# Compressed probabilities as one 128-partition tile, gate rows padded to 128 partitions, and the mLSTM's diagonal mask added by VectorE, in a hybrid mLSTM and sparse-attention block

## The chip, the core and the metric

The kernel runs on one core of a Trainium2 chip. Its metric is the device time of one execution, in microseconds (us). Before the change it is 655.17 us, the median of three runs (654.78 to 655.3).

A core has several engines that work side by side, each with its own queue: TensorE (PE in the profile) multiplies matrices and writes to PSUM; PEld is the loading of its stationary operand, which overlaps with the matmuls; VectorE (DVE), ScalarE (ACT) and GpSimd (POOL) do elementwise work; SyncE (SP) issues the DMAs. An engine works through its own instructions in the order in which they stand, and waits on semaphores for those of others.

## What is computed

One decoder layer on 512 tokens of width 1024, in float32: RMSNorm, one wide input projection, two branches, gated merge, output projection, residual, RMSNorm. Cut to what the change touches:

```python
# NSA branch, per query block: attention on 31 compressed blocks, gated with g[..., 0]
s_c = einsum('bghqd,bgnd->bghqn', qr, kc) * scale
p_c = softmax(where(m_c, s_c, NEG)) * m_c
o_c = einsum('bghqn,bgnd->bghqd', p_c, vc)
return g[..., 0:1] * o_c + g[..., 1:2] * o_s + g[..., 2:3] * o_w

# mLSTM branch, per chunk: weights of the past by gates, causal inside a chunk
logD = a[..., :, None] - a[..., None, :] + li[..., None, :]
logD = where(causal, logD, -inf)
s = einsum('bhld,bhsd->bhls', qc, kc) * exp(logD - m_t[..., None])
```

## The kernel before, in words

Nearly all products are done to float32 accuracy by splitting an operand x into a high part `h` (x rounded to float32r) and a low part `l` = x - h. `split` makes both: ScalarE copies to `h`, VectorE subtracts. A product is then three matmuls: high x high, low x high, high x low (lines 156 to 158 in `mm3`, 198, 200 and 202 in `passes`). Weights arrive by DMA in a raw tile `wr` (three buffers) and are split to `wh` and `wl` (three buffers each).

The input projection's columns run as a stream of jobs: `Stream.step(n)` gives out the next n matmuls of the current projection job, and the code calls it between the pieces of the other work, so TensorE fills with projections what would be waiting. `tick` calls it in the attention. Behind the normalisation the instructions of each engine are placed by a scheduler, by what is ready when and which buffer comes free, so that an edit can move other instructions too.

The attention runs over 4 pairs of heads, c, in two halves hh, and over two branches b (selected and window). `compressed(c)` makes the compressed scores of a head pair in `psc`, a softmax `sc` in several VectorE steps, transposes `sc` by TensorE (L735) to 64 rows (2 heads x 32 blocks) and splits the result to `pch` and `pcl`, 64 partitions each. For each of the 8 pairs (c, hh) `first` opens the output bank `po` (one buffer) with two matmuls, the compressed values `VC` (64 rows: 2 x 32; columns: high and low) against `pch` (L849) and against `pcl` (L850). Then the selected and window products come on top (L792, L793), and `collect` reads `po` with ScalarE and VectorE (`oc`).

The mLSTM runs over 4 heads. Its gates' running values lie as rows in `ghl`: rows 0 to 3 the high parts, rows 32 to 35 the low ones, of 36 partitions. A matmul with the selector `sel` of a head broadcasts a row to all 128 partitions (L946 to `pgb`). A second one (L948 to `pgm`) is followed by one (L949) that adds, with an identity `idr`, the mask `dmr` of a 128x128 diagonal block to every block. Both lie in banks of the score pool `ps`, which has two. Then seven exponentials write `Dm`: the four diagonal blocks from `pgm`, the parts behind from `pgb`. For each of four key blocks the scores are made in a bank of `ps` (L156 to L158; 512, 384, 256 and 128 columns), multiplied into `Dm` by VectorE, split to `Sh` and `Sl`, and later multiplied with the values (L979 to L981).

Of the kernel before, what the change touches and what calls it, by code (L numbers as in the profile page):

```python
# [11 lines left out]
F32 = mybir.dt.float32  # L12
F32R = mybir.dt.float32r
I32 = mybir.dt.int32
AF = mybir.ActivationFunctionType
OP = mybir.AluOpType
AX = mybir.AxisListType.X

T = 512
D = 1024  # L20
NT = T // 128
# [15 lines left out]
CI, CTRI, CROT, CCAUS, CDM, CCM, CC01, CINV, CEND = np.cumsum(  # L37
    [0, 128, 128, 128, 512, 128, 128, 128, 8]
).tolist()
# [24 lines left out]
def build(  # L64
# [22 lines left out]
    pe, pool = nc.tensor, nc.gpsimd  # L87
    act, dve = Engine(nc.scalar, "act"), Engine(nc.vector, "dve")
    A = act.activation

    pers = ctx.enter_context(tc.tile_pool(name="pers", bufs=1))
# [3 lines left out]
    def bank(tag, bufs):  # L95
        return psum.tile([128, 512], F32, name=tag, tag=tag, bufs=bufs)

    PP = lambda: bank("pp", 3)
    PS = lambda: bank("ps", 2)
# [3 lines left out]
    def f(ap):  # L103
        return ap.bitcast(F32)

    cst = pers.tile([128, CEND], F32, name="cst")
    ident = cst[:, CI : CI + 128]
# [17 lines left out]
    def split(src, hi, lo, eng="a"):  # L125
        if eng == "a":
            A(hi, src, AF.Copy)
        elif eng == "p":
            pool.tensor_scalar(hi, src, 1.0, 1.0, OP.mult, OP.mult)
        else:  # L130
            dve.tensor_copy(hi, src)
        dve.tensor_tensor(lo, src, f(hi), OP.subtract)
# [94 lines left out]
    gates = pers.tile([128, NT, 24], F32, name="gates")  # L227
    li = pers.tile([128, NT, 4], F32, name="li")
    lf = pers.tile([128, NT, 4], F32, name="lf")
    ghl = pers.tile([36, T], F32R, name="ghl")  # L230
    sel = pers.tile([36, 4], F32R, name="sel")
    Fc = pers.tile([128, NT, 4], F32, name="Fc")
    cs = pers.tile([128, NT, 4], F32, name="cs")
    em = pers.tile([128, NT, 4], F32, name="em")
# [2 lines left out]
    np_ = nsa.__enter__()  # L237
# [4 lines left out]
    rp = tc.tile_pool(name="rope", bufs=2)  # L242
    rpp = rp.__enter__()
    KC = [np_.tile([128, 2, 2, 32], F32R, name=f"KC{g}") for g in range(2)]
    VC = [np_.tile([64, 2, 2, 64], F32R, name=f"VC{g}") for g in range(2)]

    with tc.tile_pool(name="ph0", bufs=2, side="right") as p0, tc.tile_pool(
        name="small", bufs=1, side="right"
# [210 lines left out]

    for t in KC + VC:  # L460
        pool.memset(f(t), 0.0)
# [95 lines left out]
    def compress_v(hd):  # L557
        pk = PS()
        pe.matmul(pk[:64, 0:64], hd, W2[1][:, 0, :], start=True, stop=True)
        for g in range(2):  # L560
            for hh in range(2):
                s = slice(hh * 32, hh * 32 + 32)
                split(pk[g * 32 : g * 32 + 32, 0:64], VC[g][s, hh, 0, :], VC[g][s, hh, 1, :])

    KK = [[np_.tile([128, 2, T], F32R, name=f"k{g}{i}") for i in range(2)] for g in range(2)]

# [18 lines left out]
    def query_heads(c):  # L585
        H, L, a = roped.pop(("q", c))
        q = rope_b(H, L, a)
        Th = []
        for hh in range(2):
            s = slice(hh * 64, hh * 64 + 64)  # L590
            o = slice((1 - hh) * 64, (1 - hh) * 64 + 64)
            t = rpp.tile([128, T], F32R, name="Th", tag=f"Th{hh}")
            A(t[s, :], q[s, :], AF.Copy)
            dve.tensor_tensor(t[o, :], q[s, :], f(t[s, :]), OP.subtract)
            Th.append(t)
        heads[c] = H, L, Th
# [91 lines left out]
    query_heads(0)  # L688
    stream.step(8)
    compress_v(u1)  # L690
    cmp_pool.__exit__(None, None, None)

    ap_ = tc.tile_pool(name="att", bufs=2)
    at = ap_.__enter__()
# [7 lines left out]
    comp = {}  # L702

    def compressed(c):
        g = c // 2
        H, L, _ = heads[c]
        psc = PP()
        kcv = KC[g].rearrange("p i g n -> p (i g n)")
        for qb in range(NT):
            qs, o = slice(qb * 128, qb * 128 + 128), qb * 128  # L710
            pe.matmul(psc[:, o : o + 128], H[:, qs], kcv, start=True, stop=False)
            pe.matmul(psc[:, o : o + 64], L[:, qs], kcv[:, 0:64], start=False, stop=True)
        sc = at.tile([128, NT, 2, 32], F32, name="sc", tag="sc", bufs=1)
        mx = at.tile([128, NT, 2], F32, name="mx", tag="mx")
        pscv = psc.rearrange("p (b i g n) -> p b i g n", b=NT, i=2, g=2)
        dve.tensor_tensor(
            sc, pscv[:, :, 0], cm.unsqueeze(2).broadcast_to([128, NT, 2, 32]), OP.add
        )
        dve.tensor_tensor(sc, sc, pscv[:, :, 1], OP.add)
        scf = sc.rearrange("p b g n -> p (b g) n")  # L720
        mxf = mx.rearrange("p b g -> p (b g)")
        dve.tensor_reduce(mxf, scf, AX, OP.max)
        dve.tensor_tensor(scf, scf, mxf.unsqueeze(2).broadcast_to([128, 8, 32]), OP.subtract)
        A(sc, sc, AF.Exp, scale=0.125)
        dve.tensor_reduce(mxf, scf, AX, OP.add)
        dve.reciprocal(mxf, mxf)
        dve.tensor_tensor(mx, mx, gv[:, :, 2 * c : 2 * c + 2, 0], OP.mult)
        dve.tensor_tensor(scf, scf, mxf.unsqueeze(2).broadcast_to([128, 8, 32]), OP.mult)
        dve.tensor_tensor(sc, sc, c01.unsqueeze(2).broadcast_to([128, NT, 2, 32]), OP.mult)
        yield  # L730
        yield
        yield
        ptc = PP()
        for qb in range(NT):
            pe.transpose(  # L735
                ptc[:64, qb * 128 : qb * 128 + 128], sc[:, qb].rearrange("p g n -> p (g n)"), ident
            )
        pch = at.tile([64, T], F32R, name="pch", tag="pch", bufs=1)
        pcl = at.tile([64, T], F32R, name="pcl", tag="pcl", bufs=1)
        split(ptc[:64, :], pch, pcl)  # L740
        comp[c] = pch, pcl

    def softmax_block(c, hh, b, qb, pss, P, st):
        n = (qb + 1) * 128
# [64 lines left out]
    def tick(n=FILL):  # L809
        stream.step(n)  # L810
        for gen in list(side):
            if next(gen, side) is side:
                side.remove(gen)

    def new_p():
        return (
            at.tile([128, 1280], F32, name="P", tag="P", bufs=3),
            at.tile([128, 3, NT], F32, name="st", tag="st", bufs=4),
        )

    side.append(compressed(0))
    pair = new_p(), new_p()
    for qb in range(NT):
# [3 lines left out]
    po = None  # L827
    for i, (c, hh, b) in enumerate(units):
        cur = pair[b]
        if b and i + 1 < 16:  # L830
            pair = new_p(), new_p()
        if i % 4 == 2 and c < 3:
            while ("q", c + 1) not in roped:
                stream.step(1)
            query_heads(c + 1)
            side.append(compressed(c + 1))
        if i == 1:
            side.append(mgate())
        for qb in range(NT):
            if i + 1 < 16:  # L840
                score(*units[i + 1], qb, pair)
            tick()
            if late:
                late.popleft()()
        if b == 0:

            def first(c=c, hh=hh):
                vc = VC[c // 2][:, hh].rearrange("p i d -> p (i d)")
                pe.matmul(po, vc, comp[c][0], start=True, stop=False)  # L849
                pe.matmul(po, vc, comp[c][1], start=False, stop=False)  # L850

            while late:
                late.popleft()()
            po = PO()
            first()
        for kb in range(NT):
            tt = ptrans(cur[0], kb)
            tick()

            def apply(c=c, hh=hh, b=b, kb=kb, po=po, tt=tt):  # L860
                pvmul(c, b, kb, po, *tt)
                if b == 1 and kb == 3:
                    collect(c, hh, po)

            late.append(apply)
            if len(late) > LAG:
                late.popleft()()
# [14 lines left out]
    sgp = ctx.enter_context(tc.tile_pool(name="sgp", bufs=4))  # L882
    mlp = tc.tile_pool(name="ml", bufs=1)
    mp = mlp.__enter__()
    idr = mp.tile([128, 128], F32R, name="idr")
    dmr = mp.tile([128, 128], F32R, name="dmr")
    dve.tensor_copy(idr, ident)
    dve.tensor_copy(dmr, cst[:, CDM : CDM + 128])
    qk, vv = {}, {}

    def conv(i, h, e):
# [49 lines left out]
    for h in range(4):  # L941
        (qh, ql), (kh, kl) = qk[0, h], qk[1, h]
        vh, vl = vv[h]
        pgb = PS()
        sl = sel[:, h : h + 1].broadcast_to([36, 128])
        pe.matmul(pgb, sl, ghl, start=True, stop=True)  # L946
        pgm = PS()
        pe.matmul(pgm, sl, ghl, start=True, stop=False)  # L948
        pe.matmul(pgm, idr, dmr.unsqueeze(1).broadcast_to([128, 4, 128]), start=False, stop=True)  # L949
        Dm = mp.tile([128, 1280], F32, name="Dm", tag="Dm")  # L950
        for sb in range(NT):
            o, n = KOFF[sb], 512 - sb * 128
            bias = cs[:, sb, h : h + 1]
            A(Dm[:, o : o + 128], pgm[:, sb * 128 : sb * 128 + 128], AF.Exp, bias=bias, scale=-1.0)
            if n > 128:
                A(Dm[:, o + 128 : o + n], pgb[:, (sb + 1) * 128 :], AF.Exp, bias=bias, scale=-1.0)
        Sh = mp.tile([128, 1280], F32R, name="Sh", tag="Sh")
        Sl = mp.tile([128, 1280], F32R, name="Sl", tag="Sl")
        for sb in range(NT):
            o, n = KOFF[sb], 512 - sb * 128  # L960
# [13 lines left out]
        for tb in range(NT):  # L974
            po = PT()
# [152 lines left out]
```

## Time and profile before

| | |
|---|---|
| median of three runs | 655.17 us |
| span of the profiled execution, first to last instruction | 653.5 us |
| TensorE busy | 638.2 us, 3486 matmuls |
| VectorE busy | 409.1 us |
| ScalarE busy | 303.1 us |
| granted clock of TensorE, mean | 0.997 |

The page gives the profiled execution's time by its span; the runs are timed from outside, and their median is 1.7 us above that span. A busy TensorE is not one at its peak: matmuls follow each other faster than each of them lasts (a 512-column one is given some 0.4 us, but the next starts earlier), so their starts must be compared, not their durations alone. A row of a timeline is: start in us, duration in us, engine, line, operation, output tile<-input tiles, shapes, count, and in brackets the idle time before it and who ended it. Line L80 is a helper through which all VectorE and ScalarE instructions go; there the tile's name tells which it is.

### The profile page before, as it was taken

The numbers are of one execution on the slowest core, as the hardware profiler recorded it, in microseconds if no ns is written. First come the engines' busy times: TensorE is split into PE (matmuls) and PEld (weight loads), VectorE is DVE, ScalarE is ACT, GpSimd is POOL, SyncE is SP. The second block draws the span as 40 slices with busy tenths as digits, with TensorE's granted clock in tenths as the row PEclk, the third lists the DMA queues.
The fourth block names the chain that finished last, engine by engine and source line by source line (L and its number), as shares of the span: only waits on it lengthen the run. The fifth ranks groups of instructions, "written<-read, shape, count | busy, mean of one in ns | idle before, by whom it ended". The sixth has DMA issues, their size and how long they took to land.

```text
span 653.5 us, 9308 instructions
## 1 busy us (share of the span) xinstructions
PE 638.2 (98%) x3486; PEld 539.8 (83%) x3486; DVE 409.1 (63%) x874; ACT 303.1 (46%) x604; POOL 52.0 (8%) x114
## 2 busy tenths in 40 slices
PE   6999999999999999999999999999999999999996
PEld 4988778878788778888889889888888888888995
DVE  5796768757866855567579687696554233334455
ACT  5653555654655646435445546445322222223334
POOL 5000021121121221100000000000000000000000
PEclk9999999999999999999999999999999999999998
DMA  7576422122122122223212222232264242322303
GB/s 229 148 195 151 113 66 65 33 66 66 54 63 66 45 65 64 65 85 88 87 50 81 84 76 68 65 83 79 65 227 127 65 125 69 113 81 97 98 1 128
DMA packets 90125, 58.74 MB, mean 90 GB/s; under 512 B 4017, under 2 KB 86101, under 8 KB 90081
## 3 DMA queue, kind: packets, MB, share of 16 engines
q1 hardware_dynamic: 90080, 58.16, 30.8%
q8 instruction: 27, 0.44, 0.3%
q14 instruction: 18, 0.14, 0.1%
HBM read 55.01 MB, written 2.10 MB: 87 GB/s over the span
## 4 chain that ended last, share of the span: by engine, by line
PE 91%; DVE 5%; ACT 1%; DMA 1%; issue 1%; SPq 0%; POOL 0%; POOLq 0%; DVEq 0%
PE pp L198 22%; PE pp L200 22%; PE pp L202 22%; PE pp L158 3%; PE pp L156 3%; PE pp L157 3%; PE pt L780 2%; PE po L793 1%; PE po L792 1%; PE ps L765 1%; PE ps L534 1%; PE ps L766 1%; DVE wl L80 1%; DMA xt<-x 1%; PE ps L158 1%; PE ps L157 1%
## 5 line engine op out<-in xcount | busy, mean ns | idle before, releaser
L198 PE MATMUL pp<-hTh,wh 128*128 128x512 f32 (+1 forms) x488 | 194.0, 398 | 0.0
L200 PE MATMUL pp<-hTl,wh 128*128 128x512 f32 (+1 forms) x488 | 193.0, 396 | 0.0
L202 PE MATMUL pp<-hTh,wl 128*128 128x512 f32 (+1 forms) x488 | 192.5, 394 | 0.0
L80 DVE TENSOR_TENSOR wl<-wr,wh 128x1024 fp32r<-128x1024 f32 x88 | 108.6, 1235 | 88.6 <-ACT wh L80 88.1
L80 ACT ACTIVATE wh<-wr 128x1024 fp32r<-128x1024 f32 x88 | 93.1, 1059 | 119.4 <-PE pp L200 83.4
L202 PEld LDWEIGHTS pp<-hTh,wl 128*128 128x128 f32 x488 | 91.8, 188 | 17.8
L200 PEld LDWEIGHTS pp<-hTl,wh 128*128 128x128 f32 x488 | 91.9, 188 | 17.3 <-issue 0.7
L198 PEld LDWEIGHTS pp<-hTh,wh 128*128 128x128 f32 x488 | 91.8, 188 | 17.3 <-issue 0.7
L80 ACT ACTIVATE P<-P,st 128x128 f32<-128x128 f32 (+3 forms) x64 | 35.8, 559 | 37.7 <-DVE st L80 37.7
L774 POOL TENSOR_SCALAR P<-P,st 128x128 f32<-128x128 f32 (+1 forms) x64 | 36.6, 589 | 185.5 <-DVE st L80 153.0
L80 DVE CUSTOM_DVE_ANT_0 P<-ps,cst 128x128 f32<-128x128 f32 (+3 forms) x64 | 30.4, 487 | 22.4 <-PE ps L766 22.2
L80 DVE TENSOR_TENSOR ptl<-pt,pth 128x512 fp32r<-128x512 f32 (+1 forms) x64 | 30.6, 486 | 18.3 <-ACT pth L80 17.6
L80 ACT ACTIVATE pth<-pt 128x512 fp32r<-128x512 f32 (+1 forms) x64 | 27.4, 436 | 30.6 <-PE pt L780 19.2
L156 PE MATMUL pp<-wh,meh 128*128 128x256 f32 x128 | 36.2, 283 | 0.0
L157 PE MATMUL pp<-wl,meh 128*128 128x256 f32 x128 | 36.2, 283 | 0.0
L158 PE MATMUL pp<-wh,mel 128*128 128x256 f32 x128 | 36.1, 284 | 0.0
L198 PE MATMUL pp<-wh,hTh 128*128 128x256 f32 x128 | 36.0, 281 | 0.0
L80 DVE SCALAR_TENSOR_TENSOR u<-pp,prm,u 128x511 f32<-128x511 f32 (+2 forms) x48 | 35.7, 744 | 0.4
L200 PE MATMUL pp<-wl,hTh 128*128 128x256 f32 x128 | 35.9, 281 | 0.0
L202 PE MATMUL pp<-wh,hTl 128*128 128x256 f32 x128 | 35.9, 281 | 0.0
L80 DVE SCALAR_TENSOR_TENSOR s<-s,pp 128x512 f32<-128x512 f32 x16 | 11.0, 687 | 30.5 <-PE pp L202 30.5
L780 PE MATMUL pt<-cst,P 128*128 128x128 f32 x160 | 28.8, 275 | 0.0
(277 smaller groups left out, 1114.6 us busy)
## 6 DMA issues: line engine op xcount, KB each, us to landing
wr<-w_in SPq DMA_DIRECT2D x68, 512.0 KB, 3.7
wr<-w_branch_a SPq DMA_DIRECT2D x8, 512.0 KB, 3.8
wr<-w_out SPq DMA_DIRECT2D x8, 512.0 KB, 3.9
wr<-w_branch_b SPq DMA_DIRECT2D x4, 512.0 KB, 3.4
xo<-x SPq DMA_DIRECT2D x1, 2048.0 KB
out<-xo SPq DMA_DIRECT2D x8, 256.0 KB, 2.2
xt<-x SPq DMA_DIRECT2D x3, 512.0 KB, 5.8
k<-k SPq DMA_DIRECT2D x8, 128.0 KB, 2.3
```

The lines of the kernel that those rows point to most:

```text
L80: ins = fn(*args, **kw)
L156: pe.matmul(ps, a, c, start=start and i == 0, stop=False)
L157: pe.matmul(ps, a, d, start=False, stop=False)
L158: pe.matmul(ps, b, c, start=False, stop=stop and i == n - 1)
L198: pe.matmul(ps, a, c, start=k == 0, stop=False)
L200: pe.matmul(ps, a, d, start=False, stop=False)
L202: pe.matmul(ps, b, c, start=False, stop=k == nk - 1)
L534: pe.matmul(ph[:, :64], W1[i][:, j, :], Xs[i][:, j].rearrange("p g n -> p (g n)"), start=j == 0, stop=j == 15,)
L765: pe.matmul(pss[:, :n], tq, kh[:, b, :n], start=True, stop=False)
L766: pe.matmul(pss[:, :n], tq, kl[:, b, :n], start=False, stop=True)
L774: pool.tensor_scalar(pj, pj, st[:, 2, j : j + 1], 1.0, OP.mult, OP.mult)
L780: pe.transpose(pt[:, (qb - kb) * 128 : (qb - kb) * 128 + 128], P[:, POFF[qb] + kb * 128 : POFF[qb] + kb * 128 + 128], ident,)
```

## The change

The diff, shortened in nothing but its context:

```diff
-    ghl = pers.tile([36, T], F32R, name="ghl")
-    sel = pers.tile([36, 4], F32R, name="sel")
+    ghl = pers.tile([128, T], F32R, name="ghl")
+    sel = pers.tile([128, 4], F32R, name="sel")
...
-    VC = [np_.tile([64, 2, 2, 64], F32R, name=f"VC{g}") for g in range(2)]
+    VC = [np_.tile([128, 2, 2, 64], F32R, name=f"VC{g}") for g in range(2)]
...
                 split(pk[g * 32 : g * 32 + 32, 0:64], VC[g][s, hh, 0, :], VC[g][s, hh, 1, :])
+            dve.tensor_copy(VC[g][64:128], f(VC[g][0:64]))
...
-        pch = at.tile([64, T], F32R, name="pch", tag="pch", bufs=1)
-        pcl = at.tile([64, T], F32R, name="pcl", tag="pcl", bufs=1)
-        split(ptc[:64, :], pch, pcl)
-        comp[c] = pch, pcl
+        pc = at.tile([128, T], F32R, name="pc", tag="pc", bufs=1)
+        A(pc[:64], ptc[:64, :], AF.Copy)
+        dve.tensor_tensor(pc[64:128], ptc[:64, :], f(pc[:64]), OP.subtract)
+        comp[c] = pc
...
-                pe.matmul(po, vc, comp[c][0], start=True, stop=False)
-                pe.matmul(po, vc, comp[c][1], start=False, stop=False)
+                pe.matmul(po, vc, comp[c], start=True, stop=False)
...
-    idr = mp.tile([128, 128], F32R, name="idr")
-    dmr = mp.tile([128, 128], F32R, name="dmr")
-    dve.tensor_copy(idr, ident)
-    dve.tensor_copy(dmr, cst[:, CDM : CDM + 128])
+    later_only = cst[:, CDM : CDM + 128].unsqueeze(1).broadcast_to([128, NT, 128])
...
-        sl = sel[:, h : h + 1].broadcast_to([36, 128])
+        sl = sel[:, h : h + 1].broadcast_to([128, 128])
         pe.matmul(pgb, sl, ghl, start=True, stop=True)
-        pgm = PS()
-        pe.matmul(pgm, sl, ghl, start=True, stop=False)
-        pe.matmul(pgm, idr, dmr.unsqueeze(1).broadcast_to([128, 4, 128]), start=False, stop=True)
+        dg = mp.tile([128, T], F32, name="dg", tag="dg")
+        dve.tensor_tensor(
+            dg.rearrange("p (b t) -> p b t", b=NT), pgb.rearrange("p (b t) -> p b t", b=NT),
+            later_only, OP.add,
+        )
...
-            A(Dm[:, o : o + 128], pgm[:, sb * 128 : sb * 128 + 128], AF.Exp, bias=bias, scale=-1.0)
+            A(Dm[:, o : o + 128], dg[:, sb * 128 : sb * 128 + 128], AF.Exp, bias=bias, scale=-1.0)
```

The high part of the compressed probabilities lies in partitions 0 to 63 of one tile `pc`, the low part in 64 to 127; the compressed values are doubled to match, so one matmul over 128 rows adds both products. `ghl` and `sel` have 128 rows, of which the added ones are zero. The mask is added by VectorE, from PSUM into an SBUF tile `dg`.

The scheduler moves other instructions with these. On TensorE, at the beginning of the first mLSTM head (`ghl` and `sel` are the gate rows and the selector, `qkh` and `qkl` the queries and keys, `hTl` and `wh` a projection), before:

```order
L202 MATMUL pp<-wh,hTl 128x256
L946 MATMUL ps<-ghl,sel 128x512
L948 MATMUL ps<-ghl,sel 128x512
L949 MATMUL ps<-dmr,idr 128x512
L198 MATMUL pp<-hTh,wh 128x512
```

and now:

```order
L202 MATMUL pp<-wh,hTl 128x256
L943 MATMUL ps<-ghl,sel 128x512
L156 MATMUL ps<-qkh_3028,qkh_3118 128x512
L157 MATMUL ps<-qkl_3029,qkh_3118 128x512
L158 MATMUL ps<-qkh_3028,qkl_3119 128x512
```

The six matmuls of the first score block stand right behind the gate broadcast, where eight projection matmuls stood before them. Ten projection matmuls follow, and then, with what each waits for in brackets:

```order
L200 MATMUL pp<-hTl,wh 128x512
L202 MATMUL pp<-hTh,wl 128x512
L198 MATMUL pp<-hTh,wh 128x512
L156 MATMUL ps<-qkh_3028,qkh_3118 128x384 [waits DVE_49]
L157 MATMUL ps<-qkl_3029,qkh_3118 128x384
```

The second score block takes the bank of the first and waits for VectorE, which multiplies the first one into `Dm`. On VectorE, at the same place (`vl` and `wl` are low parts of values and of weights, `Sl` of the weighted scores), before:

```order
L80 TENSOR_TENSOR vl<-pp,vh 128x256
L80 TENSOR_TENSOR wl<-wr,wh 128x1024
L80 SCALAR_TENSOR_TENSOR Dm<-ps,Dm 128x512
L80 SCALAR_TENSOR_TENSOR Dm<-ps,Dm 128x384
L80 TENSOR_TENSOR Sl<-Dm,Sh 128x512
```

and now:

```order
L80 TENSOR_TENSOR vl<-pp,vh 128x256
L80 TENSOR_TENSOR dg<-ps,cst 128x512
L80 TENSOR_TENSOR wl<-wr,wh 128x1024
L80 SCALAR_TENSOR_TENSOR Dm<-ps,Dm 128x512
L80 TENSOR_TENSOR Sl<-Dm,Sh 128x512
```

The mask addition stands ahead of the weight subtraction and of the product that the second score block waits for. On ScalarE the copy `wh` of these weights now stands ahead of the seven exponentials, not behind them. On VectorE at the beginning of the attention (`ISA` on `P` and `st` is a softmax block with its row statistics, `sc` the compressed probabilities, `mx` their row scale), before:

```order
L80 ISA P,st<-ps,cst 128x512
L80 ISA st 128x1
L80 TENSOR_TENSOR sc<-sc,cst 128x256
L80 TENSOR_TENSOR wl<-wr,wh 128x1024
L80 RECIPROCAL st<-st 128x4
```

and now:

```order
L80 ISA P,st<-ps,cst 128x512
L80 ISA st 128x1
L80 TENSOR_TENSOR mx<-mx,gates 128x8
L80 TENSOR_TENSOR wl<-wr,wh 128x1024
L80 TENSOR_TENSOR sc<-sc,mx 128x256
L80 RECIPROCAL st<-st 128x4
L80 TENSOR_TENSOR sc<-sc,cst 128x256
```

The last product on `sc`, which the transposes of L735 read, stands behind the weight subtraction and a reciprocal now. The two copies that double `VC` stand some twenty instructions ahead of this, among the first softmax blocks.

## Rows read from the trace of the kernel before

**Rows 1.** The page's first part, the line of TensorE, its weight loads and the others (busy us, share of the span, instructions), and from its fourth part the shares of the engines in the chain that ended last.

```profile
PE 638.2 (98%) x3486; PEld 539.8 (83%) x3486; DVE 409.1 (63%) x874; ACT 303.1 (46%) x604; POOL 52.0 (8%) x114
...
PE 91%; DVE 5%; ACT 1%; DMA 1%; issue 1%; SPq 0%; POOL 0%; POOLq 0%; DVEq 0%
```

**Rows 2.** The groups of TensorE's matmuls by line and shape: stationary rows*columns, moving rows x columns, count, busy us, mean ns of one, idle us before them.

```profile
L198 PE MATMUL pp<-hTh,wh 128*128 128x512 f32 x472 | 189.5, 402 | 0.0
...
L849 PE MATMUL po<-pch,VC 64*128 64x512 f32 x8 | 4.0, 494 | 0.5 <-DVE oc L80 0.5
...
L850 PE MATMUL po<-pcl,VC 64*128 64x512 f32 x8 | 3.1, 391 | 0.0
...
L949 PE MATMUL ps<-dmr,idr 128*128 128x512 f32 x4 | 2.0, 498 | 0.0
L946 PE MATMUL ps<-ghl,sel 36*128 36x512 f32 x4 | 2.0, 497 | 0.0
```

**Rows 3.** The timeline of TensorE's matmuls around one of the eight compressed products (head pair 2, first half).

```profile
189.02 0.60 PE L780 MATMUL pt<-cst,P 128*128 128x128 f32 x4
189.37 0.47 PE L202 MATMUL pp<-hTh,wl 128*128 128x512 f32 x1
189.78 0.49 PE L849 MATMUL po<-pch,VC 64*128 64x512 f32 x1
190.11 0.39 PE L850 MATMUL po<-pcl,VC 64*128 64x512 f32 x1
190.44 0.50 PE L198 MATMUL pp<-hTh,wh 128*128 128x512 f32 x1
190.77 0.39 PE L200 MATMUL pp<-hTl,wh 128*128 128x512 f32 x1
191.00 0.39 PE L202 MATMUL pp<-hTh,wl 128*128 128x512 f32 x1
```

**Rows 4.** The same timeline at a compressed product that had to wait for its bank.

```profile
167.37 0.40 PE L198 MATMUL pp<-hTh,wh 128*128 128x512 f32 x1
168.01 0.50 PE L849 MATMUL po<-pch,VC 64*128 64x512 f32 x1 [0.25 <-DVE oc L80]
```

**Rows 5.** The timeline of all engines at the beginning of the first mLSTM head (weight loads and other rows left out).

```profile
317.40 0.28 PE L202 MATMUL pp<-wh,hTl 128*128 128x256 f32 x1
...
317.61 0.50 PE L946 MATMUL ps<-ghl,sel 36*128 36x512 f32 x1
317.71 0.39 ACT L80 ACTIVATE vh<-pp 128x256 fp32r<-128x256 f32 x1 [0.35 <-PE pp L202]
...
317.94 0.39 PE L948 MATMUL ps<-ghl,sel 36*128 36x512 f32 x1
318.14 2.42 ACT L80 ACTIVATE Dm<-ps,cs 128x384 f32<-128x384 f32 x7
...
318.26 0.50 PE L949 MATMUL ps<-dmr,idr 128*128 128x512 f32 x1
...
318.54 0.42 DVE L80 TENSOR_TENSOR vl<-pp,vh 128x256 fp32r<-128x256 f32 x1
318.60 0.39 PE L198 MATMUL pp<-hTh,wh 128*128 128x512 f32 x1
...
318.83 0.39 PE L200 MATMUL pp<-hTl,wh 128*128 128x512 f32 x1
...
320.42 1.09 ACT L80 ACTIVATE wh<-wr 128x1024 fp32r<-128x1024 f32 x1
...
321.55 1.23 DVE L80 TENSOR_TENSOR wl<-wr,wh 128x1024 fp32r<-128x1024 f32 x1 [2.59 <-ACT wh L80]
```

**Rows 6.** The groups of VectorE's instructions by tiles and shape, of the kinds that the change adds or removes or that a new wait hangs on (count, busy us, mean ns of one, idle us before).

```profile
L80 DVE TENSOR_TENSOR ra<-pp,Ct 128x512 f32<-128x512 f32 x6 | 4.1, 682 | 0.0
...
L80 DVE SCALAR_TENSOR_TENSOR Dm<-ps,Dm 128x512 f32<-128x512 f32 x4 | 2.7, 685 | 0.0
...
L80 DVE COPY Z<-pp 64x256 f32<-64x256 f32 x4 | 1.7, 422 | 0.2
...
L80 DVE CAST idr<-cst 128x128 fp32r<-128x128 f32 x1 | 0.3, 265 | 0.1
```

**Rows 7.** The page's line on the weight DMAs (issues, KB each, median us from issue to landing), and the two issues of SyncE on either side of the first head's start (start of the first, us to the end of the last, count).

```profile
wr<-w_in SPq DMA_DIRECT2D x68, 512.0 KB, 3.7
...
308.47 10.54 SPq L139 DMA_DIRECT2D wr<-w_in  x2
```

**Rows 8.** The timeline at the beginning of the attention: VectorE's last product on the compressed probabilities `sc`, what stands behind it, and TensorE's transposes of it.

```profile
84.25 0.69 DVE L80 CUSTOM_DVE_ANT_0 P<-ps,cst 128x512 f32<-128x512 f32 x1
...
84.86 0.42 DVE L80 TENSOR_TENSOR sc<-sc,cst 128x256 f32<-128x256 f32 x1
...
85.45 1.23 DVE L80 TENSOR_TENSOR wl<-wr,wh 128x1024 fp32r<-128x1024 f32 x1 [0.17 <-ACT wh L80]
...
86.60 0.17 DVE L80 RECIPROCAL st<-st 128x4 f32<-128x4 f32 x1
86.65 0.60 PE L735 MATMUL pp<-cst,sc 128*64 128x128 f32 x4
```

**Rows 9.** The list of waits: the matmul of L849 on VectorE's read of the output bank (us in total, times, the longest).

```profile
PE po L849 <- DVE oc L80: 0.5, 2, 0.3
```

## The prediction
> **What bounds the kernel now.** Read the page's first part, then its fourth. TensorE is busy for 638.2 us of a span of 653.5 and the chain of work that ended last runs through it for 91% [rows 1]. So a microsecond taken off TensorE is a microsecond off the kernel, unless TensorE then waits; VectorE, at 63%, counts only where TensorE stands behind it. Next comes the list of matmul shapes. A projection matmul with 128 rows and 512 columns has a mean duration of 402 ns, but the 64-row one of the compressed probabilities that comes first (L849) has 494, and the 36-row gate broadcast (L946) and the full matmul behind two of these (L949) have 497 and 498 [rows 2]. Durations overlap in a pipeline, so the price is read from starts, in a timeline of TensorE.
>
> Around a compressed product [rows 3]: undisturbed matmuls of 512 columns start 0.23 us apart (190.77 to 191.00). Here L849 to L850 takes 0.33, L850 to the projection behind it 0.33, and from that to the next another 0.33. From the transposes at 189.02 to 191.00 pass 1.98 us; four transposes at 0.11 (four of 128 columns, 0.44) and five matmuls at 0.23 would be 1.59. So the site carries about 0.39 us beyond its columns, some 0.10 at each of four starts. In a head of the mLSTM [rows 5] the same: 317.40, 317.61, 317.94, 318.26, 318.60, 318.83. That is 1.43 us for a 256-column matmul (0.12) and four of 512 (0.92): 0.39 beyond. The surcharge begins where a matmul with fewer than 128 rows begins and lasts to the first full one behind it; the full matmul L949 is slow too, as the first after the short ones.
>
> The Trainium skill, "TensorEngine Tiling (Array Packing)", section Key Properties, says that changing the tiling mode drains TensorE. The trace agrees at the ends of each site, but L849 to L850, where both have 64 rows, is slow as well, which that sentence alone would not give.
>
> **The change, part by part.**
>
> *One compressed product in place of two (8 sites).* One 512-column matmul goes (0.23), and the one that is left has 128 rows and sits between full ones. Rows 3 become 0.44 + 4 x 0.23 = 1.36 in place of 1.98: 0.62 off. Eight sites [x8 in rows 2]: 5.0 us. If only the matmul went and the surcharge stayed, 8 x 0.23 = 1.8. At two sites TensorE truly waits for the one output bank to be read (L849 idle 0.5 us in two waits [rows 9]): at the one shown, the start before it is 0.64 long [rows 4], 0.31 beyond 0.23 and 0.10. What is gained ahead of such a wait is lost in it: 0.1 each, 0.2 in all.
>
> *The split itself* keeps one ScalarE copy and one VectorE subtraction per head pair, now writing the other half of the partitions; same count and elements, taken as nothing.
>
> *The doubled compressed values (2 copies, 64 x 256, VectorE).* The nearest rows are a 128 x 128 cast at 265 ns and a 64 x 256 copy out of PSUM at 422 [rows 6]; I take 0.3 each, near the cast, since both lie in SBUF. They stand in the busiest VectorE stretch, just ahead of the first softmax blocks. There the order also moves: the 128x1024 `wl` subtraction (1.23) and a reciprocal (0.17) now come ahead of the last product of `sc`. Before, that product ended at 84.86 + 0.42 = 85.28 and TensorE came for it at 86.65 [rows 8]: 1.37 of cover. Shifted by 0.6 + 1.23 + 0.17 = 2.0 it ends at 87.28, and TensorE, with one more projection matmul ahead, comes at 86.88. It waits 0.4, with handover 0.5. Ends: 0 (VectorE catches up in a gap) and 0.9 (the dearer copy, and the other blocks late too). Later heads have no such copies.
>
> *The gate rows padded to 128 and the mask taken off TensorE (4 heads).* Two 512-column matmuls go and the third becomes a full one: rows 5 become 0.12 + 2 x 0.23 = 0.58 in place of 1.43, 0.85 off, 3.4 us for four heads. Without the surcharge 4 x 2 x 0.23 = 1.8. The two casts for `idr` and `dmr` [rows 6] went on VectorE with no one shown waiting: nothing.
>
> *The mask on VectorE.* Each head adds a 128x512 addition from PSUM, 682 ns like `ra` [rows 6], so 2.7 us of VectorE that has room. What counts is the wait it adds. With one score bank freed, the first score block moves up in front of the projections, and the second (128x384) now waits for VectorE's product of the first, whose bank it takes over. Take 317.40 of rows 5 as zero point, and let TensorE go on without the surcharge: gate matmul at 317.52, six score matmuls, ten projections, so the second block is reached at 317.52 + 17 x 0.23 = 321.4. VectorE: `vl` ends at 318.96, the mask at 319.64, `wl` behind it (1.23) at 320.87, the product of block one (685 ns [rows 6]) at 321.56. ScalarE is in time for both: `vh` ends at 318.10, `wh` (1.09) now stands ahead of the exponentials and ends at 319.2, before the mask is there; the first two of the seven exponentials (2.42 for all seven) are done by about 320.6. So TensorE waits 0.1 to 0.2, with handover; I take 0.15, 0.6 for four heads. Below, it could be nothing (a VectorE step a little quicker), above, 0.4 per head if ScalarE's exponentials end later than the `wl` subtraction. The remaining blocks have over a microsecond each: between their first matmuls lie at least 1.4 us of TensorE work (six of 384 columns or projections), and a VectorE product of 384 is under 0.69.
>
> **Sum.** -5.0 - 3.4 = -8.4; back come 0.2 + 0.5 + 0.6 = 1.3. Net -7.1. The profiled execution's span of 653.5 becomes 646.4; the runs' median is 655.17, 1.7 above the span for what lies around it, and that does not change: 655.17 - 7.1 = 648.1 us.
>
> **Rivals.**
>
> *A. The surcharge is not one of rows.* It might belong to the change of bank and accumulation group, and stay. Then only 16 matmuls go: 16 x 0.23 = 3.7, less the 1.3: 652.8. For it: L949 has 128 rows and is slow. Against it: the first projection behind, 318.60 to 318.83, goes at 0.23 again although its group is new too, and L949 stands right behind the 36-row ones.
>
> The Trainium skill, "TensorE: Matmul & The Clock Gate", section Why this matters for your kernels, says that a single matmul with 32 contraction rows takes the same time as one with 128, so padding would give nothing: by it the time is A's. Rows 2 and 3 speak against it in a stream of mixed row counts, since the same 512 columns there take 0.33.
>
> *B. VectorE and ScalarE give the pace in attention.* Then gains at sites ahead of a wait vanish, as in rows 4. If half of the 5.0 goes that way and the upper prices hold (0.9 at the start, 0.4 per head): 8.4 - 2.5 - 0.9 - 1.6 = 3.4, time 651.8. For it: the two waits; 5% of the chain is VectorE's [rows 1]. Against it: TensorE's idle time there is 0.5 us in all [rows 9].
>
> *C. The mLSTM slows, and the kernel is slower than before.* The product of block one stands behind `wl`, and `wl` behind `wh`, and `wh` behind the landing of its weights. If they are late, TensorE stands still in every head, where before the exponentials and scores did not sit behind that transfer. It decides from (8.4 - 0.7) / 4 = 1.9 us per head: `wh` would have to end at 321.5, not 319.2. With one whole median landing, 3.7 us [rows 7], added to the 318.1 at which ScalarE reaches it, `wh` ends at 322.9, 3.7 late, 3.5 of it on the path: four heads lose 14 and the time is about 661. Against it: of the two transfers of rows 7 one was issued at 308.47, ten microseconds before it is needed.
>
> **Chances.** Forecast 0.76 (own range 646.7 to 649.7: the gain without losses, 655.2 - 8.4, and with the upper prices at the start, in the heads and two more waited sites), A 0.07, B 0.14, C 0.03. The time should lie in 646.3 to 651.6, which leaves out A, C and a part of B. A measurement of this kernel tells 0.2% (1.3 us) from no change. Faster by more than that: the forecast, A and most of B, 0.94; within it 0.03; slower 0.03.
>
> **What would show it.** Starts 0.23 apart around the line of the compressed product and around the gate broadcast, with a mean duration near 400 ns in both, prove the row count; 0.33 proves A. The first transposes of `sc` should come about half a microsecond late, and the 384-column score block should show a wait on VectorE's `Dm` of 0.1 to 0.2 in each head; over 1 us there would be C's way. TensorE's busy time should fall by about 7. If the sites speed up and the time does not follow, B is right, and the waits on `oc` and `ptl` will have grown.

## The result, and the profile after

The changed kernel takes 649.4 us (median of 4 runs, 648.97 to 650.03), the kernel before on the same chip 655.07 (654.78 to 655.3). The ratio is 0.9914, with a 95% interval from 0.9902 to 0.9926: 5.7 us faster. The forecast was 648.1, with its own range from 646.7 to 649.7. A second measurement of the changed kernel, later, gave 649.54 against 655.35, ratio 0.9907 (0.9893 to 0.9922).

First the page of the changed kernel, its first part and the chain's shares by engine (as [rows 1]):

```profile
PE 632.3 (98%) x3470; PEld 538.4 (83%) x3470; DVE 412.2 (64%) x878; ACT 302.8 (47%) x604; POOL 54.0 (8%) x114
...
PE 90%; DVE 6%; ACT 2%; DMA 1%; issue 1%; SPq 0%; POOL 0%; DVEq 0%; POOLq 0%
```

TensorE lost 16 matmuls and 5.9 us of busy time, the span 5.3 (648.2 against 653.5). This one execution took 650.03, 0.6 above the median; its first projection matmuls start 0.65 us later than in the execution profiled before, ahead of everything that was changed. So stages are compared here, not spans.

Matmuls by shape (as [rows 2]; stationary rows*columns, moving rows x columns, count, busy us, mean ns, idle us before them). The gate broadcast's own mean can be read in the timeline further down; the score product L156 is the first full one behind it.

```profile
L850 PE MATMUL po<-pc,VC 128*128 128x512 f32 x8 | 3.8, 472 | 0.5 <-DVE oc L80 0.5
...
L156 PE MATMUL ps<-qkh,qkh 128*128 128x512 f32 x8 | 3.2, 400 | 0.0
```

The compressed product is still dear, 472 ns; the first full matmul behind the gate broadcast is not, 400 where L949 had 498. The timeline shows why. TensorE at the site of [rows 3]:

```profile
188.90 0.48 PE L202 MATMUL pp<-hTh,wl 128*128 128x512 f32 x1
189.28 0.50 PE L850 MATMUL po<-pc,VC 128*128 128x512 f32 x1
189.61 0.40 PE L198 MATMUL pp<-hTh,wh 128*128 128x512 f32 x1
189.85 0.39 PE L200 MATMUL pp<-hTl,wh 128*128 128x512 f32 x1
```

Behind the product the projections go at 0.23 again; before, the first one still took 0.33. But the start ahead of it takes 0.38 and its own 0.33. At the site of [rows 4] the same, with a wait that the profile names (PEld is the weight load of the product):

```profile
167.34 0.40 PE L198 MATMUL pp<-hTh,wh 128*128 128x512 f32 x1
167.98 0.19 PEld L850 LDWEIGHTS po<-pc,VC 128*128 128x128 f32 x1 [0.67 <-DVE oc L80]
167.98 0.50 PE L850 MATMUL po<-pc,VC 128*128 128x512 f32 x1 [0.24 <-DVE oc L80]
...
168.31 0.40 PE L200 MATMUL pp<-hTl,wh 128*128 128x512 f32 x1
```

And the first mLSTM head (all engines; as [rows 5], other rows left out). 315.64 answers to 317.40 there:

```profile
315.64 0.28 PE L202 MATMUL pp<-wh,hTl 128*128 128x256 f32 x1
...
315.76 0.40 PE L943 MATMUL ps<-ghl,sel 128*128 128x512 f32 x1
...
316.00 0.40 PE L156 MATMUL ps<-qkh,qkh 128*128 128x512 f32 x1
...
316.24 0.40 PE L157 MATMUL ps<-qkl,qkh 128*128 128x512 f32 x1
...
317.12 0.68 DVE L80 TENSOR_TENSOR dg<-ps,cst 128x512 f32<-128x512 f32 x1
...
317.71 1.21 DVE L80 TENSOR_TENSOR wl<-wr,wh 128x1024 fp32r<-128x1024 f32 x1
...
318.85 0.68 DVE L80 SCALAR_TENSOR_TENSOR Dm<-ps,Dm 128x512 f32<-128x512 f32 x1
...
319.49 0.40 PE L198 MATMUL pp<-hTh,wh 128*128 128x512 f32 x1
...
319.73 0.34 PE L156 MATMUL ps<-qkh,qkh 128*128 128x384 f32 x1
```

315.64, 315.76, 316.00, 316.24: the columns and nothing beyond. The masked block's product is done at 319.53, and TensorE comes for its bank at 319.73, 0.24 behind the projection ahead, without a wait.

Two stages hold the gain. The attention, from the start of its first score block to the first gate broadcast, took 317.61 - 78.54 = 239.06 us before and 315.76 - 79.10 = 236.66 after, 2.4 less. Three mLSTM heads, from the first gate broadcast to the fourth, took 446.77 - 317.61 = 129.16 and 442.33 - 315.76 = 126.57, 0.86 less for each, 3.5 for four. Together 5.9. The same two numbers from the traces of the experiments are the table that the next section refers to:

```
us                                  attention   three heads
before                                239.06       129.16
compressed part alone                 236.72       129.15
mLSTM part alone                      238.99       126.58
padding alone, tiles anew             237.44       128.17
changed kernel                        236.66       126.57
changed kernel, measured again        236.68       126.56
+ copies of VC on GpSimd              236.12       126.59
+ product behind the value products   234.86       126.56
gate rows 64                          236.75       127.70
gate rows 96                          236.70       126.55
gate rows 64, three times             236.79       129.15
```

### The profile page after: what moved, and what is told of

It is laid out like the page before. It is cut to its first block, busy times and chain, and to the rows that moved or that the text cites. A ratio compares the mean times of both kernels' runs of the same rounds, so it can differ in the third digit from the quotient of the medians.

```text
span 648.2 us, 9274 instructions
## 1 busy us (share of the span) xinstructions
PE 632.3 (98%) x3470; PEld 538.4 (83%) x3470; DVE 412.2 (64%) x878; ACT 302.8 (47%) x604; POOL 54.0 (8%) x114
## 4 chain that ended last, share of the span: by engine, by line
PE 90%; DVE 6%; ACT 2%; DMA 1%; issue 1%; SPq 0%; POOL 0%; DVEq 0%; POOLq 0%
PE pp L200 22%; PE pp L198 22%; PE pp L202 22%; PE pp L158 3%; PE pp L156 3%; PE pp L157 3%; PE pt L781 2%; DVE wl L80 1%; PE po L794 1%; PE ps L766 1%; PE po L793 1%; PE ps L534 1%; PE ps L767 1%; ACT wh L80 1%; DMA xt<-x 1%; PE ps L157 1%
## 5 line engine op out<-in xcount | busy, mean ns | idle before, releaser
L202 PE MATMUL pp<-hTh,wl 128*128 128x512 f32 (+1 forms) x488 | 192.5, 394 | 0.0
L202 PEld LDWEIGHTS pp<-hTh,wl 128*128 128x128 f32 x488 | 91.7, 188 | 17.9
L775 POOL TENSOR_SCALAR P<-P,st 128x128 f32<-128x128 f32 (+1 forms) x64 | 38.7, 625 | 182.6 <-DVE st L80 147.1
L156 PE MATMUL pp<-wh,meh 128*128 128x256 f32 x128 | 36.2, 283 | 0.0
L157 PE MATMUL pp<-wl,meh 128*128 128x256 f32 x128 | 36.2, 283 | 0.0
L202 PE MATMUL pp<-wh,hTl 128*128 128x256 f32 x128 | 35.9, 281 | 0.0
```

What stands on the lines that cost most here:

```text
L156: pe.matmul(ps, a, c, start=start and i == 0, stop=False)
L157: pe.matmul(ps, a, d, start=False, stop=False)
L202: pe.matmul(ps, b, c, start=False, stop=k == nk - 1)
L775: pool.tensor_scalar(pj, pj, st[:, 2, j : j + 1], 1.0, OP.mult, OP.mult)
```

## The experiments

**The two parts alone.** Each kernel holds one part of the diff and leaves the other as it was: the compressed part alone has the changes of `VC`, `pc` and the product of L849 and L850, the mLSTM part alone those of `ghl`, `sel`, `idr`, `dmr` and `dg`.

> Only the compressed probabilities as one tile of 128 rows; the mLSTM is that of before. Theory (the site gains are real, but a part of them runs into VectorE's read of the one output bank and into the softmax blocks): about 2.3 us gained, 652.8, with the full matmuls around L850 0.23 us apart and 3.9 us gained in the eight sites. Rival 1 (the prediction's sum: 5.0 less 0.2 and 0.5): 650.8. Rival 2 (the surcharge is not of rows, only eight matmuls go): 655.1 - 1.8 + 0.7 = 654.0.

> Only the gate rows padded to 128 and the mask moved to VectorE; the attention is that of before, two 64-row products at each site. Theory (surcharge of rows, no wait on the masked block): 0.85 us a head, 3.4 to 3.5 in all, 651.6, head period 42.2 us. Rival 1 (two matmuls a head and nothing else): 1.8, 653.3. Rival 2 (the two parts are not independent, the gain in the mLSTM comes from how the attention ends): anything that does not add with the run of the other part to the 5.7 of the whole change.

Measured 653.13 (ratio 0.9963, 0.9951 to 0.9976) and 652.28 (0.9952, 0.9940 to 0.9965), beside 655.6 before. The shares, 0.37% and 0.48%, add to 0.85%, and the whole change has 0.86%. In the table each part moves its own stage by the whole amount and the other by less than 0.1. So the shortfall against the forecast lies in the attention alone.

**Padding alone.** Is it the row count, or the matmuls that went? Here none goes: the operands are filled with zeros to 128 rows, and both compressed products, both gate matmuls and the mask stay on TensorE.

```diff
-    ghl = pers.tile([36, T], F32R, name="ghl")
+    ghl = pers.tile([128, T], F32R, name="ghl")
...
-        pch = at.tile([64, T], F32R, name="pch", tag="pch", bufs=1)
...
+    pch = np_.tile([128, T], F32R, name="pch")
...
+        pool.memset(f(t), 0.0)
```

> No matmul is removed: both compressed products, both halves of the gate broadcast and the mask stay on TensorE; only the rows of their operands are filled up with zeros to 128. Theory (the surcharge belongs to matmuls of fewer rows and to the first full one behind them): starts 0.23 apart at both places, 0.39 gained in each of four heads (1.6), and up to 0.39 at each of eight sites, less what the waits on the output bank keep: 1.6 to 2.4 of 3.1; time 651 to 652.5. Rival (the surcharge is of bank and accumulation group): starts stay at 0.33, time 655.1 or a little above for the memory fills and the copies.

Measured 654.66 (0.9983, 0.9974 to 0.9992). With one pair of padded tiles for all head pairs, the second half's product takes the next pair's probabilities and so has to wait for them: this kernel computes something else, the product's place in the order moved, and its attention can't be read against before. The heads don't hang on it, and the experiment was made again with tiles taken anew for each head pair:

```diff
+            pool.memset(f(VC[g][64:128]), 0.0)
...
+        pch = at.tile([128, T], F32R, name="pch", tag="pch", bufs=1)
...
+        pool.memset(f(pch[64:128]), 0.0)
```

> As the run that only pads, but with the two zero-padded tiles of the compressed probabilities taken anew for each head pair, as in the kernel before; the order of TensorE's instructions is that of before, row for row, and no matmul is removed. Theory (surcharge of rows): 0.39 less in each of four heads (1.6), the sites' starts 0.23 apart where TensorE doesn't wait for the output bank, and there 0.39 less (sites 1, 6, 7, 8) or 0.1 to 0.2 less (2 to 5), 2.0 to 2.3 in all; time before less 3 to 4 us. Rival (the gain of the changed kernel in the attention is of the removed matmuls alone): before less 1.6.

Measured 652.45 (0.9954, 0.9939 to 0.9968), 3.15 us less than before with every matmul still there. TensorE at the site of [rows 3] (L852 and L853 are the two products), and at the gate broadcast (L949 and L951, with the mask in L952):

```profile
189.43 0.50 PE L852 MATMUL po<-pch,VC 128*128 128x512 f32 x1
189.77 0.39 PE L853 MATMUL po<-pcl,VC 128*128 128x512 f32 x1
190.00 0.39 PE L198 MATMUL pp<-hTh,wh 128*128 128x512 f32 x1
...
316.46 0.40 PE L949 MATMUL ps<-ghl,sel 128*128 128x512 f32 x1
316.70 0.39 PE L951 MATMUL ps<-ghl,sel 128*128 128x512 f32 x1
316.93 0.39 PE L952 MATMUL ps<-dmr,idr 128*128 128x512 f32 x1
317.16 0.39 PE L198 MATMUL pp<-hTh,wh 128*128 128x512 f32 x1
```

Same banks, same accumulation groups, same order, and 0.23 in place of 0.33, but for the start behind L852, which opens the bank right behind VectorE's read of it: the surcharge belongs to the rows. Rival A is out. In the table padding takes 0.33 off each head (the four starts around the gate broadcast give 0.39, a few hundredths are lost again later in the head) and 1.6 off the attention. Removing the eight products then takes only 0.8 more, of 8 x 0.23 = 1.8; 0.55 of what is missing is the start of the attention, where the changed kernel copies VC and this one doesn't (below).

**How many rows, and how many matmuls.** The changed kernel with 64 gate rows, with 96, and with the 64-row broadcast issued three times into the same bank.

```diff
-    ghl = pers.tile([128, T], F32R, name="ghl")
+    ghl = pers.tile([64, T], F32R, name="ghl")
...
+        for _ in range(3):
             pe.matmul(pgb, sl, ghl, start=True, stop=True)
```

> The changed kernel with gate rows of 64 partitions in place of 128 (the rest as it is). If a matmul of 64 rows is dear as the 36-row one was: the start before the gate broadcast, its own and the one behind it each 0.1 longer, 0.3 per head, 1.2 in all. If 64 rows are as good as 128: 0.23 between the starts, no change. If it is the narrow product in a row of narrow ones that is dear, not a single one: no change either, and the mean duration stays near 400 ns.

> As the run with 64 rows, with 96. If every count under 128 pays: 0.33 at the gate broadcast, 1.2 us in all, as with 64. If only up to 64 pays (half of the rows): 0.23 and no change against the changed kernel.

> As the run with gate rows of 64 partitions, but the gate broadcast is issued three times in a row into the same bank. The surcharge around one 64-row matmul was 0.39 us a head, the same as around the two 36-row ones of the kernel before. If it is the price of going into and out of narrow matmuls: again 0.39 beyond the columns, so 0.46 us more a head than with one (two times 0.23). If it is a price of each narrow matmul: 0.6 to 0.8 beyond the columns.

One run each: 651.08 with 64 rows, 648.58 with 96, 652.91 with 64 rows three times. TensorE around the gate broadcast with 64 rows:

```profile
315.16 0.28 PE L202 MATMUL pp<-wh,hTl 128*128 128x256 f32 x1
315.37 0.50 PE L943 MATMUL ps<-ghl,sel 64*128 64x512 f32 x1
315.79 0.50 PE L156 MATMUL ps<-qkh,qkh 128*128 128x512 f32 x1
316.13 0.40 PE L157 MATMUL ps<-qkl,qkh 128*128 128x512 f32 x1
```

with 96:

```profile
314.22 0.28 PE L202 MATMUL pp<-wh,hTl 128*128 128x256 f32 x1
314.34 0.40 PE L943 MATMUL ps<-ghl,sel 96*128 96x512 f32 x1
314.58 0.40 PE L156 MATMUL ps<-qkh,qkh 128*128 128x512 f32 x1
```

with 64 rows three times:

```profile
315.11 0.28 PE L202 MATMUL pp<-wh,hTl 128*128 128x256 f32 x1
315.32 0.96 PE L944 MATMUL ps<-ghl,sel 64*128 64x512 f32 x3
316.21 0.50 PE L156 MATMUL ps<-qkh,qkh 128*128 128x512 f32 x1
316.55 0.40 PE L157 MATMUL ps<-qkl,qkh 128*128 128x512 f32 x1
```

From L202 to L157 pass 0.97 us with one narrow matmul and 1.44 with three. The columns between are worth 0.12 + 2 x 0.23 = 0.58 and 0.12 + 4 x 0.23 = 1.04; beyond them 0.39 and 0.40. In [rows 5], with two narrow ones, it was 0.39. So the surcharge doesn't grow with the number of narrow matmuls: it is paid once, about half on the way in and half on the way out. And 96 rows pay nothing: the step lies between 64 and 96. Single runs can't tell times this near to each other apart, but the heads in the table bear it out: against the changed kernel a head is 0.38 longer with 64 rows, not longer with 96, and 0.86 longer with three 64-row matmuls (0.39 + 2 x 0.23 = 0.85).

The weight loads show where it is paid. With 64 rows:

```profile
315.37 0.18 PEld L943 LDWEIGHTS ps<-ghl,sel 64*128 64x128 f32 x1
315.79 0.19 PEld L156 LDWEIGHTS ps<-qkh,qkh 128*128 128x128 f32 x1 [0.25 <-issue]
315.90 0.19 PEld L157 LDWEIGHTS ps<-qkl,qkh 128*128 128x128 f32 x1
```

Between full matmuls a load starts well ahead of its own matmul (L157: 315.90 against 316.13). The loads of the first narrow and of the first full one start only with their matmul (315.37, 315.79): nothing runs ahead that would hide them.

**Where the attention lost its share: the copies of VC.** GpSimd makes them instead of VectorE.

```diff
-            dve.tensor_copy(VC[g][64:128], f(VC[g][0:64]))
+            pool.tensor_scalar(VC[g][64:128], f(VC[g][0:64]), 1.0, 1.0, OP.mult, OP.mult)
```

> The changed kernel with the copies of VC made by GpSimd, not VectorE. Theory (the two copies of 0.29 us ahead of the first softmax blocks make TensorE wait at the start of attention): the wait at the first score block of head 0 (0.74 us between L200 and L766) falls by 0.3 to 0.5 and the time to 649.0. Rival (the wait comes from the order, in which the subtraction of wl and a reciprocal now stand ahead): the wait stays and so does 649.4. Third: GpSimd is later than VectorE and the first compressed product waits for VC: slower than 649.4.

Measured 648.88 (0.9903, 0.9889 to 0.9916). All engines at the first softmax blocks in the changed kernel:

```profile
80.31 0.29 DVE L80 CAST VC<-VC 64x256 fp32r<-64x256 f32 x1
...
80.58 0.40 PE L200 MATMUL pp<-hTl,wh 128*128 128x512 f32 x1
...
80.63 0.21 DVE L80 TENSOR_TENSOR VC<-ps,VC 32x64 fp32r<-32x64 f32 x1
...
80.87 0.29 DVE L80 CUSTOM_DVE_ANT_0 P<-ps,cst 128x128 f32<-128x128 f32 x1
...
81.32 0.36 PE L766 MATMUL ps<-k,Th 128*128 128x256 f32 x1 [0.34 <-DVE st L80]
```

TensorE at the same place with the copies on GpSimd:

```profile
79.71 0.39 PE L198 MATMUL pp<-hTh,wh 128*128 128x512 f32 x1
80.00 0.36 PE L766 MATMUL ps<-k,Th 128*128 128x256 f32 x1
```

The second softmax block (`P`, 80.87) stands behind a copy and behind a subtraction for VC that moved ahead of it with the copy (80.63), and the score block that needs its bank starts 0.74 behind the projection ahead; with the copies moved, and that subtraction behind the softmax block again, it is 0.29. The table gives 0.55 for the attention. With the copies moved, the subtraction of `wl` also stands behind the last product of `sc` again, so this run undoes the moved order too; but in the changed kernel `wl` starts at 85.81, over four microseconds behind this wait, which so is that of the copies and of what moved with them. The medians of the two kernels, taken at different times, are too near each other to tell them apart; the stage and the row do.

**Where it lost its share: the one output bank.** Two ways to take away the wait on VectorE's read (`oc`), both with the copies on GpSimd. First a second bank, taken from the projections:

```diff
-    PP = lambda: bank("pp", 3)
+    PP = lambda: bank("pp", 2)
-    PO = lambda: bank("po", 1)
+    PO = lambda: bank("po", 2)
```

> The changed kernel with the copies of VC on GpSimd and one of the three banks of pp given to po, so that two output banks alternate. Theory (TensorE waits at sites 2 to 5 for VectorE's read of the one output bank): these waits, 0.57 + 0.17 + 0.59 + 0.17 us beyond the columns in the profile of the changed kernel, go, and 1.0 to 1.5 us are gained on the 648.9 of the run with the copies on GpSimd. Rival 1 (VectorE sets the pace there): they come back at the next score block or at ptl, 648.9. Rival 2: with two pp banks the projections or the compressed scores wait for a bank, slower than 648.9.

Measured 662.82 (1.0110, 1.0096 to 1.0125), slower than before. Around seven of the eight products the starts are 0.23 apart, and the wait on `oc` is gone at all of them, but TensorE now waits for the projections' banks (the list of TensorE's waits: us in total, times, longest):

```profile
PE pp L198 <- DVE Z L80: 2.7, 1, 2.7
PE pp L198 <- ACT s L80: 2.5, 1, 2.5
```

Behind these two waits the granted clock fell: on the mean it is 0.66 from 45 to 50 and from 83 to 88 us, and 1.00 up to 45, between the two and from 88 to 660. So TensorE had the lower of the clock's two levels (1.2 GHz) for a part of each stretch; in the 5 and the 3 us before, it had been busy for 2.3 and 1.0. With a third of the clock gone over 5 us twice, this cost some 3.4 us, as an estimate. The scheduler also chose another order: the attention takes 228.83 us and three heads 134.36, so work moved from one stage to the other, and the rest of the 14 us over the run with the copies alone is not divided further here. Then no bank is moved; the product is issued behind the first two value products of its half, and these open the bank:

```diff
+        lead = b == 0 and kb == 0
+        pe.matmul(po[:, kb * 128 :], vl, th[:, :n], start=lead, stop=False)
...
+        if lead:
+            pe.matmul(po, vc, comp[c], start=False, stop=False)
```

> The changed kernel with the copies of VC on GpSimd, and the compressed product issued behind the first two value products of a half instead of ahead of them, so that the first matmul into the output bank comes several transposes and projections later; no bank is moved. Theory (TensorE waits at sites 2 to 5 for VectorE's read of the one output bank): the waits go, 1.0 to 1.5 us less than the run with the copies on GpSimd alone, 1.5 to 2.0 less than the changed kernel. Rival (VectorE sets the pace there, and the wait comes again at the next score block or the next ptl): no less than 0.4 to 0.5 under the changed kernel, the copies' share.

> The changed kernel once more, for a comparison on one chip with the next run: 0.9914 of before, 649 to 650.

Measured 647.82 (646.88 to 648.4; ratio to before 0.9885, 0.9869 to 0.9902) beside 649.54 (649.0 to 649.84) for the changed kernel on the same chip: 1.7 us less. TensorE at the site of [rows 4]:

```profile
168.76 0.39 PE L794 MATMUL po<-pth,vsw 128*128 128x512 f32 x1
168.99 0.39 PE L795 MATMUL po<-ptl,vsw 128*128 128x512 f32 x1
169.22 0.40 PE L798 MATMUL po<-pc,VC 128*128 128x512 f32 x1
169.46 0.28 PE L760 MATMUL ps<-k,Th 128*128 128x256 f32 x1
```

No wait for `oc` is left in its list of waits, and the table gives 1.26 us for the attention over the copies alone. This is the best of the kernels here.

## Why the prediction was right, and where it was off

**The forecast case came in the total, in part by luck.** Faster by 5.7 against 7.1 forecast, inside the forecast's own range. But the heads gained 3.5 where 3.4 - 0.6 = 2.8 was forecast, and the attention 2.4 where 5.0 - 0.2 - 0.5 = 4.3 was. The two misses partly cancel: had the 0.6 come that was put down to the masked block, the time would have been 650.0, above that range. TensorE's busy time fell by 5.9, not 7.

**Gate rows and mask: 3.4, measured 3.5.** Two matmuls a head and the surcharge of 0.39: 0.85 was worked out, 0.86 came. Padding alone has 0.33 of it in the table, the other 0.53 came with the two removed matmuls and the moved mask (0.46 by the columns).

**The wait on the masked block: 0.6 forecast, none came.** Counted from the last short projection, VectorE's product was expected at +4.16 (321.56 - 317.40) and TensorE at +4.0; they came at 319.53 - 315.64 = +3.89 and 319.73 - 315.64 = +4.09. VectorE was a quarter of a microsecond quicker through mask, `wl` and product, because these follow each other with less between them than their durations say (317.12, 317.71, 318.85: `wl` starts 0.09 before the mask's duration is over). The prediction had named nothing as the lower end, "a VectorE step a little quicker"; that is what came. Rival C, the mLSTM behind late weights, had nothing in it.

**The eight sites: 5.0 less 0.2; this is the term that was mis-sized.** Beyond the columns (0.23 for 512, 0.11 for a transpose) TensorE's starts around the eight sites, from the second ahead of the products to the second behind, held 3.7 us before and 1.6 after, worked out from the timeline; with the eight products gone, 1.8, the sites gained 3.9, not 4.8. The step that failed is "What is gained ahead of such a wait is lost in it: 0.1 each, 0.2 in all": two named waits were counted, but at four sites, the second to the fifth, TensorE stood before the bank, and 1.4 of the 1.6 lie there. At 168 us the start ahead of L850 is 0.64 long, as before, and its own 0.33. The site of [rows 3], whose 0.62 was taken for all eight, is itself one of the four: from the projection ahead of the product to the second one behind passed 190.77 - 189.37 = 1.40 us before and 189.85 - 188.90 = 0.95 after, 0.45 less. Before, part of the wait lay there under the surcharge. [rows 9] names only the waits of matmuls; the weight loads of the same line, in the same list of the kernel before, waited for the same read seven times:

```profile
PEld po L849 <- DVE oc L80: 2.6, 7, 0.7
```

The kernel with the product behind the value products gets this back (1.26 us), which shows it.

**The start of the attention: 0.5, right size, wrong place.** The prediction expected TensorE to wait at the transposes of `sc`, behind the copies and the moved `wl`. It waits 0.45 more (0.74 against 0.29) a step sooner, at the second score block, for a softmax block behind a copy of VC (0.29 us each, as taken) and a subtraction of 0.21 that moved with it, and the run with the copies on GpSimd gives 0.55 back. By then TensorE itself was late enough that the transposes cost it nearly nothing: they start at 87.94, 0.27 behind the projection ahead.

**What remains of rival B.** The sites gained 3.9 and the attention 2.4. Of the 1.5 between, 0.45 is the second score block; two more starts grew, each at VectorE:

```profile
192.94 0.40 PE L198 MATMUL pp<-hTh,wh 128*128 128x512 f32 x1
193.62 0.33 PE L781 MATMUL pt<-cst,P 128*128 128x128 f32 x1 [0.28 <-DVE ptl L80]
...
222.65 0.40 PE L198 MATMUL pp<-hTh,wh 128*128 128x512 f32 x1
223.23 0.41 PE L766 MATMUL ps<-k,Th 128*128 128x384 f32 x1 [0.18 <-DVE st L80]
```

0.68 and 0.58 where 0.23 are usual, 0.8 together. The rest, some 0.3, is in smaller places that were not followed up. So a TensorE that runs faster between VectorE's results waits for them a little more, as B said, and `ptl` and `oc` are the waits that it named: that on `ptl` is new, 0.3 in the list of TensorE's waits, while that on `oc` stayed at 0.5. In the attention alone B's sum, 5.0 - 2.5 - 0.9 = 1.6, was nearer to the 2.4 than the forecast's 4.3. In the whole kernel its price was too high: the sites lost 0.9 of the forecast, not 2.5, and the heads nothing where it put 1.6.

**The surcharge's mechanism was misread, its size was right.** The prediction put about 0.10 at each of four starts, as a price of short matmuls and of the first full one. The runs with one and three narrow matmuls show a price for the change from full to narrow and back, 0.39 for the pair however many narrow ones lie between; with two of them the four slow starts happen to be all there are, and L849 to L850 is slow as the start behind the first narrow one. Had one narrow matmul been left at each place (no padding), that reading would have forecast 0.3 for each, and 0.39 would have stayed. The Trainium skill, "TensorEngine Tiling (Array Packing)", Key Properties, says that changing the tiling mode drains TensorE; the prediction held L849 to L850 against that rule, but the runs agree with it in so far as the price comes with the change, 0.39 for one and 0.40 for three narrow matmuls. The drain itself no trace here shows. The same page, Available Configurations, lists row tiles of 32, 64 and 128 rows and none between; the runs agree, with 0.39 at 64 rows and nothing at 96.

## What to carry to other kernels

Look in TensorE's timeline for starts that are longer than the columns around a matmul of 64 rows or fewer in a stream of full ones: here each such place in the mLSTM cost 0.39 us, and filling the rows with zeros took that away at no cost on TensorE (3.15 us in this kernel, attention and mLSTM together, with nothing removed). Before counting a gain ahead of a matmul that opens an accumulation bank, look when the last reader of that bank ends, and for waits of its weight load as well as its own; issue first into the bank what comes latest anyway. A copy of 0.29 us on an engine that TensorE waits for cost 0.45, with what the scheduler moved along with it, where it stood just ahead of what was waited for.

## What the runs showed of the hardware

- The price of going from full to narrow matmuls and back is 0.39 us, the same for one, two and three narrow ones in between, 36 or 64 rows (0.39, 0.39, 0.40).
- A moving operand of 96 rows costs no more than one of 128: starts 0.24 and 0.23 apart.
- A full matmul that opens a bank just behind its last reader carries about 0.1 more in the start behind it too (0.33 at 167.98 and at 189.28), although its rows are full; where nothing reads the bank just before, it is 0.24 (169.22 to 169.46). In the trace its weight load starts only with the matmul itself (167.98), as those around narrow matmuls do; no run was made to tell whether this is the cause.
- On VectorE, an instruction can start before the time given for the one ahead is over (the mask at 317.12 for 0.68, `wl` at 317.71), so sums of durations run a little long.
